# Order of the background work in a decoder step: selections ahead of row products, two groups of sparse tokens, a later first product

## The chip, the core and the metric

The kernel runs on one core of a Trainium2 chip. The core has five engines with a queue of instructions each: TensorE (PE, matrix products; PEld is its weight load), VectorE (DVE), ScalarE (ACT), GpSimd (POOL) and SyncE (SP, which here only issues DMAs). Each takes its queue strictly in order; semaphores hold an instruction until what it needs is done. All DMAs, issued from the queues of SP, ACT and POOL, run on 16 DMA engines. The metric is the device time of one execution in microseconds; the median of several is given. "Half" below is one step of the kernel's main loop, explained there.

## The reference

One layer of a decoder is computed for 256 prompt tokens and 8 sample tokens (264 columns). The part that matters is the PEER layer behind the first normalization: each token's query scores two sets of 128 keys for each of 8 heads, the best 16 pairs of a head choose 16 of 16384 single-neuron experts, and

```python
def block(args):
    xb, ib, gb = args
    hid = jax.nn.gelu(jnp.einsum('td,thkd->thk', xb, u_tab[ib]).astype(jnp.float32), approximate=False)
    coef = (gb * hid).astype(xb.dtype)
    return jnp.einsum('thk,thkd->td', coef, v_tab[ib])
```

So a token takes 8 x 16 = 128 rows of `u_tab` and 128 rows of `v_tab`, each of 2048 floats. Ahead of it come the mixers (an SSD scan, a short convolution, branch gates, an output projection), behind it a second normalization and a gated projection.

## The kernel before

**The main loop.** Everything with a weight matrix runs through one list, `order`, of weight tiles of 128 x 1024 floats: "halves". For each half SP loads the tile (`fetch`, L135), ACT rounds it to fp32r (`whi`, L146) and DVE takes the rest (`wlo`, L147), and PE multiplies with both. Loads go out four halves ahead and splits three halves ahead (`next_half`). Stage by stage: 24 column blocks of convolution inputs, the short convolution, the gates, the output projection, the queries; then **u**, 128 blocks of two halves, which multiplies the first 216 tokens with all 16384 experts' u rows (L271 to L274, `pair_block`); then **v**, 8 chunks of 16 blocks of two halves, which multiplies the coefficients of all experts with the v rows; then the last projection.

**Two ways through PEER.** The first 216 tokens (TD) are computed densely: all 16384 hidden values, times a gate that is zero where an expert isn't chosen. The last 48 (NSP: 40 prompt tokens and the 8 samples) are computed sparsely: only their chosen rows are gathered from HBM. Both need the selection first.

**The background planner.** What isn't the main loop is written as Python generators in a list, `tasks`, whose place in it is their rank. Behind each half the kernel calls `tick(budget)`. A tick first runs what was deferred to it (`defer`), then goes through `tasks` in order: a task that isn't waiting may emit work as long as the credit is above zero; `yield 2.4` takes 2.4 credits, `yield ("w", n)` lets it wait for n ticks. Credit comes back by the budget at each tick (1.1 in u, 1.0 in v) and may run below zero. So the planner sets, at build time, at which half each instruction enters its engine's queue; the engines then work through the queues. `Grid` spaces the steps of a task: at least n ticks behind the last step's planned time, and at least one tick from now.

**The tasks of this case**, all started around the queries' end:

- `token_rows` transposes x1 of the 48 sparse tokens to rows and writes them to HBM (`x1_d`).
- `select_all` runs three selections (`select`): tile 0, the prompt tokens 128 to 255; tile 1, the 8 samples, laid out as 64 rows of token and head; tile 2, the prompt tokens 0 to 127. Selections are DVE work: sums of candidates, top 16 (L1040 to L1044), lookups (`big`, L1071 to L1076). Behind tiles 0 and 1 `send` writes the chosen rows' numbers and weights of the sparse tokens to HBM (L1132). Behind tile 0 the task `gates(128, 88)` is put at the head of the list, and at the very end `select_all` itself goes on as `gates(0, 128)`, once the first gates are done (L1111 to L1113).
- `gates` builds, four tokens a step and a step every three halves, two one-hot matrices: four POOL instructions (L1151) and one of DVE (L1152); six halves later PE multiplies them (`gps`, L1164) and ACT copies the result to `gs`. Behind 32 tokens SP writes `gs` (2 MB) to HBM (L1156).
- `sparse_experts` runs through 96 jobs: for each group of tokens, first the u rows, then the v rows. Job by job POOL gathers 128 rows (`ug`, L1188, two buffers, the next job's gather ahead of a product), and a product on DVE follows every four halves: for u the dot products with `x1s` (L1216), for v the sum into `x1s` (L1226). Ahead of a group's first product `x1s` must be filled: the group's n token rows, 128/n times (L1207); `x1s` has one buffer, which the group before gives up only when PE has folded its 128 partial sums to n tokens (`yS`, L1232). `index` loads a tile's row numbers from HBM.
- Behind the last gates, `to_v` frees the selection's buffers and starts `residual` (copies for v's accumulators) and `prep(0)`: for each of a chunk's four blocks, load gates and hidden values, multiply, split into `co` (L1301 to L1311). v's first chunk needs all four; later chunks are prepared beside the one before, and what is left of `prep` at a chunk's start is run out without matmuls between. Before the last chunk the kernel emits what is left of `sparse_experts` (L1395), since its result enters the second normalization.

The sparse tokens form three groups, `GR`: 32 prompt tokens, 8 prompt tokens, and the 8 samples. When tile 0 is sent, `sparse_experts` is put at the head of `tasks`, so that from then on products rank above `select_all`. Job 32 (the first v row of the first group) waits until tile 1 is sent, and loads its index.

Of the kernel before, what the change touches and what calls it, by code (L numbers as in the profile page):

```python
# [10 lines left out]
F = mybir.dt.float32  # L11
R = mybir.dt.float32r
U32 = mybir.dt.uint32
# [6 lines left out]
NS = 8  # L20
T = PT + NS
TW = T + 2
NSP = 48
# [7 lines left out]
PH = 8  # L31
TOPK = 16
# [13 lines left out]
TB = 32  # L46
NB, TR = divmod(TD, TB)

GR = ((0, 32, 0, 88, 32), (32, 8, 0, 120, 8), (40, 8, 1, 0, 64))


@with_exitstack
def hybrid_step(ctx: ExitStack, tc: tile.TileContext, xT, pT, w_in, w_dt, w_bs, w_bc, w_o, w_q, w_pg, w_pp,
                uT, vP, uR, vR, keysT, par, hpar, hist, h0, eye, tri, iota, fold, yT, o_hp, o_hs, o_cp, o_cs, o_sp, o_ss):
    nc = tc.nc
    te, ve, ac, gp, sy = nc.tensor, nc.vector, nc.scalar, nc.gpsimd, nc.sync
# [4 lines left out]
    dram = ctx.enter_context(tc.tile_pool(name="dram", bufs=1, space=bass.MemoryType.DRAM))  # L61
# [36 lines left out]
    def bank(name, tag="bg", bufs=4):  # L98
        return psum.tile([128, 512], F, name=name, tag=tag, bufs=bufs)
# [12 lines left out]
    sidx = cpool.tile([128, NSP], U32, name="sidx")  # L112
    scf = cpool.tile([128, NSP], F, name="scf")
# [38 lines left out]
    tasks = []  # L152
    later = []
    clock = {"t": 0, "credit": 0.0, "in": False}

    def defer(n, fn):
        later.append((clock["t"] + n, fn))
# [31 lines left out]
    def spawn(gen):  # L189
        tk = {"gen": gen, "wait": 0}  # L190
        tasks.append(tk)
        return tk
# [130 lines left out]
    for q in range(6):  # L323
        n = min(3, 16 - 3 * q)
# [8 lines left out]
        for s in range(n):  # L333
            h, l = split_block(xt[:, s * T:(s + 1) * T], "x")
# [622 lines left out]
    DONE = {}  # L957
# [130 lines left out]
    def select_all():  # L1088
        while sum(h in DONE for h in range(PH)) < PH:
            yield ("w", 1)  # L1090
        t2_stack.close()
        sp = P["sp"] = sp_stack.enter_context(tc.tile_pool(name="select", bufs=1))
        P["oh"] = oh_stack.enter_context(tc.tile_pool(name="onehot", bufs=1))
        for t, (t0, n, nh) in enumerate(TT):
            sel = sp.tile([128, 3, nh * TOPK], F, name=f"sel{t}")
            yield from select(t, sel)
            if t < 2:
                send(sel, t, nh)
            if t == 0:
                tasks.insert(0, {"gen": sparse_experts(), "wait": clock["t"] + 1})  # L1100
            if t != 1:
                nd = min(n, TD - t0)
                yield ("w", 2)
                ps = bank("slt")
                for q in range(3):
                    te.transpose(ps[:, q * 128:q * 128 + n], sel[:n, q], ident[:n, :n])
                for q in range(3):
                    ac.copy(slot[q][:, t0:t0 + nd], ps[:, q * 128:q * 128 + nd])
                if t == 0:
                    tasks.insert(0, {"gen": gates(t0, nd), "wait": clock["t"] + 1})  # L1110
        while "G" + str(PT // 2) not in DONE:  # L1111
            yield ("w", 1)
        yield from gates(0, PT // 2)  # L1113


    sx_d = [dram.tile([128, n], U32, name=f"sx{g}_d") for g, (_, n, _, _, _) in enumerate(GR)]
    sg_d = [dram.tile([128, n], F, name=f"sg{g}_d") for g, (_, n, _, _, _) in enumerate(GR)]
    x1_d = dram.tile([NSP, D], F, name="x1_d")

    def send(sel, t, nh):  # L1120

        sp = P["sp"]
        ix = sp.tile([128, nh * TOPK], U32, name=f"ix{t}")
        fx = sp.tile([128, nh * TOPK], F, name="fx", tag="fx", bufs=1)
        n = TT[t][1]
        ve.scalar_tensor_tensor(fx[:n], sel[:n, 0], 128.0, sel[:n, 1], OP.mult, OP.add)
        ve.tensor_copy(ix[:n], fx[:n])
        for g, (_, m, tile_, lo, r) in enumerate(GR):
            if tile_ == t:
                c = nh * TOPK // m  # L1130
                for d, src in ((sx_d[g], ix), (sg_d[g], sel[:, 2])):
                    gp.dma_start(out=bass.AP(tensor=d.tensor, offset=d.offset, ap=[[m, r], [r * m, c], [1, m]]),  # L1132
                                 in_=src[lo:lo + r].rearrange("p (c m) -> p c m", m=m))
        DONE["sent%d" % t] = True

    GS = {}

# [40 lines left out]
        gp.dma_start(out=x1_d, in_=xr[:NSP])  # L1178

    def sparse_experts():  # L1180
        jobs = [(tab, k0, n, c) for k0, n, _, _, _ in GR for tab in (uR, vR) for c in range(k0, k0 + n)]
        rows = {}

        def get(i):
# [4 lines left out]
                                      in_offset=bass.IndirectOffsetOnAxis(ap=sidx[:, c:c + 1], axis=0))  # L1189
                rows[i] = t  # L1190

        def index(t):
            for g, (k0, n, tile_, _, _) in enumerate(GR):
                if tile_ == t:
                    gp.dma_start(out=sidx[:, k0:k0 + n], in_=sx_d[g])
                    gp.dma_start(out=scf[:, k0:k0 + n], in_=sg_d[g])

        yield ("w", 1)
        index(0)
# [2 lines left out]
        for i, (tab, k0, n, c) in enumerate(jobs):  # L1202
            ks = slice(k0, k0 + n)
            if tab is uR and c == k0:
                x1s = lp.tile([128, D], F, name="x1s", tag="x1s", bufs=1)
                for q in range(128 // n):
                    gp.dma_start(out=x1s[q * n:(q + 1) * n], in_=x1_d[ks])  # L1207
            if i == 32:
                while "sent1" not in DONE:
                    yield ("w", 1)  # L1210
                index(1)
            get(i + 1)
            yield grid(STEP)
            t = rows.pop(i)
# [256 lines left out]
def _inputs(x_prompt, x_sample, p_prompt, p_sample, state_ssm, state_ssd_conv, state_shortconv,  # L1471
# [34 lines left out]
        iota=np.tile(np.arange(128, dtype=np.float32), (128, 1)),  # L1506
        fold=np.concatenate([np.tile(np.eye(g[1]), (128 // g[1], 1)) for g in GR], 1).astype(np.float32),
    )
# [33 lines left out]
```

## Time and profile before

| | |
|---|---|
| median of 3 runs | 2680.55 us (2678.95 to 2682.51) |
| profiled execution | 2681.55 us, its span 2679.8 us |
| granted clock of TensorE, mean | 0.984 |
| packets of DMA | 677.84 MB, 253 GB/s over the span |
| gathers of `ug` | 48 of u rows, median 8.7 us to landing; 48 of v rows, 9.2 us |
| loads of weights in u and v | 256 of 512 KB each, 5.4 and 5.9 us |

The u stage lies about from 1150 to 1860 us of the span, v from there to 2500 us. The page gives busy times and idle times of engines; the windows view gives them for stretches of the span, also for one line alone, where the counts (x) tell how fast that line went; the waits view tells who waited for whom; the timeline gives single instructions, in square brackets how long their engine was idle before and what ended that.

### The profile page before, as it was taken

The page shows a single profiled execution, that of the slowest core. Times are in us where ns is not written, and L with a number is a line of the kernel's source. Part 1 is how long each engine was busy: PE and PEld are TensorE (multiplying, and loading weights), DVE is VectorE, ACT ScalarE, POOL GpSimd, SP SyncE. Part 2 cuts the span into 40 slices and gives each one's busy share as a digit, 9 for nine tenths or more (in the row PEclk, how much of TensorE's full clock was granted, in tenths as well). Part 3 has the DMA queues.
Part 4 walks back from the last instruction along what each step waited for, and adds up shares of the span by engine and source line. Part 5 has one row for each costly group of instructions (what it writes and reads, how often), then busy time and mean ns, then how long its engine had stood idle before and what let it go on. Part 6 is the DMA issues. An engine that isn't in the chain of part 4 may idle for free.

```text
span 2679.8 us, 48780 instructions
## 1 busy us (share of the span) xinstructions
PE 2605.1 (97%) x18999; PEld 2549.7 (95%) x18999; DVE 2039.8 (76%) x3258; ACT 1343.0 (50%) x1894; POOL 739.7 (28%) x802
## 2 busy tenths in 40 slices
PE   8999999999999999999999999997889989999999
PEld 8999999999999999999899999997779989999999
DVE  7899865566445577899788887776869978877886
ACT  5665533454334445655565565555434434444563
POOL 2232200000000010100699478784332332100100
PEclk9999999999999999999999999998889999999999
DMA  6798756556666666667898998889879989887664
GB/s 229 225 298 265 246 166 181 182 174 183 180 182 181 180 181 174 176 203 207 264 326 328 349 334 328 330 334 342 331 268 366 378 310 366 308 267 243 204 197 136
DMA packets 202041, 677.84 MB, mean 253 GB/s; under 512 B 23712, under 2 KB 61216, under 8 KB 188192
## 3 DMA queue, kind: packets, MB, share of 16 engines
q1 hardware_dynamic: 156128, 509.65, 58.7%
q0 software_dynamic: 27664, 146.49, 15.1%
q10 hardware_dynamic: 18016, 18.58, 2.0%
q8 instruction: 148, 2.42, 0.4%
q14 instruction: 85, 0.70, 0.1%
HBM read 633.72 MB, written 40.90 MB: 252 GB/s over the span
## 4 chain that ended last, share of the span: by engine, by line
PE 82%; POOL 6%; DMA 5%; DVE 4%; issue 2%; ACT 1%; SPq 0%; DVEq 0%; ACTq 0%; POOLq 0%
PE mm L271 22%; PE mm L237 15%; PE mm L235 15%; PE mm L236 15%; PE mm L272 11%; POOL o L1151 5%; DMA w<-uT 2%; PE mm L274 1%; DVE wlo L147 1%; PE gps L1164 1%; DMA x1s<-x_d 1%; POOL ug L1188 1%; DMA ug<-uR,sidx 1%; DMA al<-a_d 1%; PE yS L1232 0%
## 5 line engine op out<-in xcount | busy, mean ns | idle before, releaser
L147 DVE TENSOR_TENSOR wlo<-w,whi 128x1024 fp32r<-128x1024 f32 x916 | 1115.9, 1223 | 405.9 <-ACT whi L146 401.3
L146 ACT CAST whi<-w 128x1024 fp32r<-128x1024 f32 x916 | 961.0, 1051 | 841.5 <-PE mm L236 289.6
L271 PE MATMUL mm<-co,whi 128*128 128x432 f32 x1920 | 613.8, 377 | 23.4 <-DVE co L1311 15.1
L271 PE MATMUL mm<-x,whi 128*128 128x432 f32 x1920 | 610.4, 375 | 1.1 <-ACT whi L146 1.1
L237 PE MATMUL mm<-x,wlo 128*128 128x264 f32 x1920 | 550.0, 286 | 2.7 <-DVE wlo L147 2.7
L235 PE MATMUL mm<-x,whi 128*128 128x264 f32 x1920 | 549.7, 286 | 1.5 <-ACT whi L146 1.5
L236 PE MATMUL mm<-x,whi 128*128 128x264 f32 x1920 | 547.3, 285 | 0.0
L272 PE MATMUL mm<-co,wlo 128*128 128x216 f32 x2048 | 524.6, 266 | 14.8 <-DVE wlo L147 14.8
L272 PE MATMUL mm<-x,wlo 128*128 128x216 f32 x2048 | 521.3, 265 | 14.8 <-DVE wlo L147 14.7
L272 PEld LDWEIGHTS mm<-co,wlo 128*128 128x128 f32 x2048 | 397.6, 194 | 17.4 <-DVE wlo L147 15.6
L272 PEld LDWEIGHTS mm<-x,wlo 128*128 128x128 f32 x2048 | 393.7, 192 | 21.0 <-DVE wlo L147 19.0
L271 PEld LDWEIGHTS mm<-co,whi 128*128 128x128 f32 x1920 | 368.3, 192 | 42.8 <-DVE co L1311 16.5
L271 PEld LDWEIGHTS mm<-x,whi 128*128 128x128 f32 x1920 | 364.0, 190 | 17.6 <-ACT whi L146 1.5
L235 PEld LDWEIGHTS mm<-x,whi 128*128 128x128 f32 x1920 | 363.6, 189 | 3.2 <-ACT whi L146 1.8
L237 PEld LDWEIGHTS mm<-x,wlo 128*128 128x128 f32 x1920 | 362.4, 189 | 3.1 <-DVE wlo L147 3.1
L236 PEld LDWEIGHTS mm<-x,whi 128*128 128x128 f32 x1920 | 363.6, 189 | 0.0
L1151 POOL TENSOR_SCALAR o<-iot,slot,slot 128x128 f32<-128x128 f32 x216 | 354.1, 1646 | 1.6
L1216 DVE SCALAR_TENSOR_TENSOR ug<-ug,x1s 128x2048 f32<-128x2048 f32 x48 | 110.3, 2297 | 44.2 <-DMA x1s<-x_d 31.8
L1188 POOL DMA_INDIRECT ug<-vR,sidx x48 | 78.7, 1640 | 219.9 <-DVE x1s L1226 167.5
L833 POOL CAST r1h<-r1gbh 128x2 fp32r<-128x2 f32 x16 | 5.2, 326 | 476.3 <-PE mm L237 476.3
L1188 POOL DMA_INDIRECT ug<-uR,sidx x48 | 72.7, 1514 | 162.1 <-DVE ug L1216 133.6
L1226 DVE SCALAR_TENSOR_TENSOR x1s<-ug,scf,x1s 128x2048 f32<-128x2048 f32 x45 | 105.5, 2345 | 2.7 <-DMA ug<-vR,sidx 2.7
(350 smaller groups left out, 3864.3 us busy)
## 6 DMA issues: line engine op xcount, KB each, us to landing
w<-uT SPq DMA_DIRECT2D x256, 512.0 KB, 5.4
w<-vP SPq DMA_DIRECT2D x256, 512.0 KB, 5.9
w<-w_in SPq DMA_DIRECT2D x240, 512.0 KB, 3.9
w<-w_bc SPq DMA_DIRECT2D x32, 512.0 KB, 3.7
w<-w_bs SPq DMA_DIRECT2D x32, 512.0 KB, 3.6
w<-w_o SPq DMA_DIRECT2D x32, 512.0 KB, 3.6
w<-w_q SPq DMA_DIRECT2D x32, 512.0 KB, 3.6
w<-w_pg SPq DMA_DIRECT2D x32, 512.0 KB, 4.3
```

The lines of the kernel that those rows point to most:

```text
L146: ac.copy(hi, w)
L147: ve.tensor_tensor(lo, w, hi.bitcast(F), OP.subtract)
L235: te.matmul(ps, wh, xh[kb], start=(first and q == 0), stop=False)
L236: te.matmul(ps, wh, xl[kb], start=False, stop=False)
L237: te.matmul(ps, wl, xh[kb], start=False, stop=(last and q == n - 1))
L271: te.matmul(ps, hi[:, ws], xp[kb], start=(kb == 0), stop=False)
L272: te.matmul(ps[:, :TD], lo[:, ws], xp[kb][:, :TD], start=False, stop=False)
L274: te.matmul(ps, hi[:, ws], xp[kb], start=False, stop=True)
L1151: gp.tensor_scalar(o1[:, q], iot, slot[0][:, c], slot[2][:, c], OP.is_equal, OP.mult)
L1188: gp.indirect_dma_start(out=t, out_offset=None, in_=tab, in_offset=bass.IndirectOffsetOnAxis(ap=sidx[:, c:c + 1], axis=0))
L1216: ve.scalar_tensor_tensor(t, t, 1.0, x1s, OP.mult, OP.mult, accum_out=shid[:, c:c + 1])
L1226: ve.scalar_tensor_tensor(x1s, t, scf[:, c:c + 1], x1s, OP.mult, OP.add)
```

## The change

Three things, in the planner's inputs and in the way the indices travel:

1. `sparse_experts` is appended to `tasks` instead of put at the head, so it ranks below `select_all` and, when they come, above `prep`. The first gates are still put at the head.
2. `GR` has two groups, 32 and 16 tokens. The second holds 8 prompt tokens and the 8 samples. Its row numbers come from two tiles into one tensor of HBM: the prompt tokens' part is written at once by POOL (as before), the samples' part by 16 DMAs on SP's queue (8 heads, numbers and weights), deferred by two ticks behind tile 1's selection. `index(1)` then loads the whole second group.
3. Behind the loads of `x1s` the generator waits four ticks before it goes on to the next gather and the first product.

```diff
-GR = ((0, 32, 0, 88, 32), (32, 8, 0, 120, 8), (40, 8, 1, 0, 64))
+GR = ((0, 32), (32, 16))
...
             if t == 0:
-                tasks.insert(0, {"gen": sparse_experts(), "wait": clock["t"] + 1})
+                spawn(sparse_experts())
...
-        for g, (_, m, tile_, lo, r) in enumerate(GR):
-            if tile_ == t:
-                c = nh * TOPK // m
-                for d, src in ((sx_d[g], ix), (sg_d[g], sel[:, 2])):
-                    gp.dma_start(out=bass.AP(tensor=d.tensor, offset=d.offset, ap=[[m, r], [r * m, c], [1, m]]),
-                                 in_=src[lo:lo + r].rearrange("p (c m) -> p c m", m=m))
-        DONE["sent%d" % t] = True
+
+        def rows(eng, g, tok, src, stride, runs, m):
+            for d, x in ((sx_d[g], ix), (sg_d[g], sel[:, 2])):
+                eng.dma_start(out=bass.AP(tensor=d.tensor, offset=d.offset + tok * m,
+                                          ap=[[m, len(src)], [stride, runs], [1, m]]),
+                             in_=x[src.start:src.stop].rearrange("p (c m) -> p c m", m=m))
+
+        if t == 0:
+            for g, (k0, m) in enumerate(GR):
+                lo = n - (NSP - NS) + k0
+                src = range(lo, min(lo + m, n))
+                rows(gp, g, 0, src, m * m, 128 // m, m)
+        else:
+            g, m = len(GR) - 1, GR[-1][1]
+
+            def later_rows():
+                for h in range(PH):
+                    rows(sy, g, h * m + m - NS, range(h * NS, h * NS + NS), m * m, 1, m)
+                DONE["sent"] = True
+
+            defer(2, later_rows)
...
-        def index(t):
-            for g, (k0, n, tile_, _, _) in enumerate(GR):
-                if tile_ == t:
-                    gp.dma_start(out=sidx[:, k0:k0 + n], in_=sx_d[g])
-                    gp.dma_start(out=scf[:, k0:k0 + n], in_=sg_d[g])
+        def index(g):
+            k0, n = GR[g]
+            gp.dma_start(out=sidx[:, k0:k0 + n], in_=sx_d[g])
+            gp.dma_start(out=scf[:, k0:k0 + n], in_=sg_d[g])
...
                 for q in range(128 // n):
                     gp.dma_start(out=x1s[q * n:(q + 1) * n], in_=x1_d[ks])
+                yield ("w", 4)
             if i == 32:
-                while "sent1" not in DONE:
+                while "sent" not in DONE:
                     yield ("w", 1)
                 index(1)
```

More of the change, by code (lines that the diff above doesn't have):

```diff
@@ L1113, in select_all @@
         yield from gates(0, PT // 2)
-    sx_d = [dram.tile([128, n], U32, name=f"sx{g}_d") for g, (_, n, _, _, _) in enumerate(GR)]
-    sg_d = [dram.tile([128, n], F, name=f"sg{g}_d") for g, (_, n, _, _, _) in enumerate(GR)]
+    sx_d = [dram.tile([128, n], U32, name=f"sx{g}_d") for g, (_, n) in enumerate(GR)]
+    sg_d = [dram.tile([128, n], F, name=f"sg{g}_d") for g, (_, n) in enumerate(GR)]
     x1_d = dram.tile([NSP, D], F, name="x1_d")
@@ L1180, in sparse_experts @@
     def sparse_experts():
-        jobs = [(tab, k0, n, c) for k0, n, _, _, _ in GR for tab in (uR, vR) for c in range(k0, k0 + n)]
+        jobs = [(tab, k0, n, c) for k0, n in GR for tab in (uR, vR) for c in range(k0, k0 + n)]
         rows = {}
```

## The prediction

> **What bounds the kernel now.** I read the page first: busy shares, the 40 slices, the chain.
>
> ```profile
> span 2679.8 us, 48780 instructions
> PE 2605.1 (97%) x18999; PEld 2549.7 (95%) x18999; DVE 2039.8 (76%) x3258; ACT 1343.0 (50%) x1894; POOL 739.7 (28%) x802
> PE   8999999999999999999999999997889989999999
> PE 82%; POOL 6%; DMA 5%; DVE 4%; issue 2%; ACT 1%; SPq 0%; DVEq 0%; ACTq 0%; POOLq 0%
> L272 PE MATMUL mm<-x,wlo 128*128 128x216 f32 x2048 | 521.3, 265 | 14.8 <-DVE wlo L147 14.7
> ```
>
> PE bounds the kernel nearly everywhere, so a change in the background order can only pay where PE stands still: the slices with 7 and 8 behind the middle. To find these places I count one line. Each weight half of the u and v stages holds eight matmuls of L272 (2048 in the 256 halves of u). The windows view of that line alone, in 50 us stretches, is a speedometer (the last columns are granted clock, DMA share, GB/s):
>
> ```profile
> 1300.00:1350.00 50.00, 32.07 (x122) 24.56 (x123) 0.93 0.86 290
> 1400.00:1450.00 50.00, 35.98 (x143) 27.11 (x143) 1.00 0.87 301
> 1500.00:1550.00 50.00, 40.10 (x160) 30.27 (x159) 1.00 0.99 370
> 1850.00:1855.00 5.00, 2.51 (x8) 1.95 (x8) 0.82 1.02 407
> 1855.00:1860.00 5.00, 3.63 (x13) 3.04 (x14) 0.84 1.01 385
> 1850.00:1900.00 50.00, 16.67 (x53) 14.18 (x54) 0.62 0.85 314
> 1950.00:2000.00 50.00, 31.80 (x123) 24.27 (x122) 0.90 0.79 272
> 2000.00:2050.00 50.00, 33.85 (x129) 26.12 (x129) 0.90 0.89 327
> 2100.00:2150.00 50.00, 40.92 (x163) 30.82 (x162) 1.00 0.98 378
> 2150.00:2200.00 50.00, 31.38 (x120) 24.04 (x120) 0.90 0.82 293
> ```
>
> Undisturbed, v does 163 per 50 us, so a half takes 2.45 us, even with the DMA engines at 0.98. With gate matmuls between, u does 143, so three halves take 8.4 us. The places that are short: **A**, 1300 to 1350, (143-122)/143 x 50 = 7.3 us; **B**, 1850 to 1900, (163-53)/163 x 50 = 33.7 us; **C**, 1950 to 2050, (40+34)/163 x 50 = 22.7 us; **D**, 2150 to 2200, 13.2 us. In all 77 us, the clock's half speed after each stop included.
>
> Next I asked what PE waits for there, with the waits view and the timeline:
>
> ```profile
> DVE ug L1216 <- DMA x1s<-x_d: 8.4, 1, 8.4
> DVE ug L1216 <- DMA x1s<-x_d: 23.4, 2, 12.2
> 1987.44 5.71 POOL L1207 DMA_DIRECT2D x1s<-x_d  x11 [15.02 <-PE yS L1232]
> 1995.42 2.83 POOL L1207 DMA_DIRECT2D x1s<-x_d  x5 [2.28 <-DMA x1s<-x_d]
> 2004.06 2.29 DVE L1216 SCALAR_TENSOR_TENSOR ug<-ug,x1s 128x2048 f32<-128x2048 f32 x1 [11.25 <-DMA x1s<-x_d]
> 1869.25 0.70 PE L271 MATMUL mm<-co,whi 128*128 128x432 f32 x1 [8.30 <-issue]
> 1878.37 0.73 PE L271 MATMUL mm<-co,whi 128*128 128x432 f32 x1 [6.53 <-DVE co L1311]
> 1886.06 0.73 PE L271 MATMUL mm<-co,whi 128*128 128x432 f32 x1 [5.06 <-DVE co L1311]
> 1891.98 0.73 PE L271 MATMUL mm<-co,whi 128*128 128x432 f32 x1 [3.29 <-DVE co L1311]
> ```
>
> A, C and D are one thing three times: a group's first product stands on VectorE before its x1s has landed (8.4 us in u; 23.4 us for the two later groups, the first row from 1250 to 1550, the second from 1850 to 2330). VectorE works in order, so the weight splits (L147) queue behind that product, and PE runs dry. B is the passage from u to v: PE takes up v's first four coefficient blocks one by one, as L1311 delivers them, because their preparation begins only when the last gate is written.
>
> **The change part by part.** Positions are halves of u and v (256 each), counted by the planner's rules: 1.1 credits per half of u, 1.0 in v.
>
> *Rank.* A selection of eight heads costs 1.1 + 8 x 0.95 + 1.4 + 4 x 3.4 + 0.8 = 24.5 credits, the small one 6.65. The first ends at half 51 in both kernels. Before, the remaining 31.2 credits share the halves with 22 gate steps (15.4) and 22 products (52.8): 99.4 / 1.1 = 90 halves, so selection ends at 144. The gates of the first tile are done at 121 (22 steps of 3 halves), and those of the second, 32 x 3 = 96 halves, run from 148 to 244. With the write and its deferral `to_v` comes at 250, six halves before u ends: only the first of the four co blocks is begun in u. After, no product runs before the selections end: (31.2 + 12 x 0.7) / 1.1 = 36 halves, so half 89. Now the first tile's gates are last, at 120; the second's follow at once and end at 216, and `to_v` comes at 222. `prep` takes 8 halves a block beside the products: multiplies at 227, 235, 243 and 251, last co at 255, u's end at 256. So B's wait goes. The trace shows the hole that closes, in the windows view of L1151:
>
> ```profile
> 1450.00:1500.00 50.00, 37.31 (x17) 1.00 0.92 345
> 1500.00:1550.00 50.00, 0.00 (x0) 1.00 0.99 370
> 1550.00:1600.00 50.00, 34.60 (x19) 1.00 0.94 335
> ```
>
> From 1500 to 1550 POOL builds no gate at all: it waits for the selection. What stays of B is the cost of the last gate write, seen in 1850 to 1860 as 10 - 21/3.26 = 3.6 us (3.26 is 163/50), now near half 222, and about 1 us at the boundary. **B gains 33.7 - 3.6 - 1 = 29.**
>
> *The wait of four halves.* The first product of a group now comes five halves behind its loads, 12.3 us. Behind the waiting generator nothing is queued on an engine; it only emits later. For A the loads go out near half 59 and the product at 89, so that wait goes entirely. **A gains 6** (7.3, less about 1 for POOL, held for the index at half 59, below).
>
> *Two groups for three.* One transition goes, with its 16 loads, its fold and its gelu; the other has 8 loads of 128 KB for 16 of 64 KB.
>
> ```profile
> x1s<-x_d POOLq DMA_DIRECT2D x32, 64.0 KB, 5.5
> x1s<-x_d POOLq DMA_DIRECT2D x4, 256.0 KB, 11.1
> L1232 PE MATMUL yS<-fld,x1s 128*128 128x8 f32 x32 | 3.6, 253 | 0.0
> ```
>
> Eight issues take 8 x 0.52 = 4.2 us (5.71 for eleven), with no pause as behind the eleventh. A landing of 128 KB is between 5.5 and 11.1; I take 5.5 as nearer (64 KB), so 9.7 us, inside 12.3. At 11.1 it is 15.3, 3 us late, about a half that the splits made ahead mostly hide. The transition falls at half 337, inside a chunk, where before both fell on chunk boundaries. Left are the fold's 3.6 us and some 1.3. **C and D gain 35.9 - 3.6 - 1.3 = 31.** The 96 products are the same; the last group ends at half 457 for 416, and the last chunk, which needs it, starts at 480. With products v runs 163 per 50 us, so 41 more such halves cost nothing.
>
> *The row writes on SP.* At half 63 sixteen DMAs of 512 bytes stand before weight loads on SP's queue. Nearest rows:
>
> ```profile
> L643 SPq DMA_DIRECT2D h0t<-h x64: 378/384/874, 84.3 to 295.5; - x64
> SPq L1156 <- ACT gs L1165: 40.0, 6, 7.4
> g_d<-gs SPq DMA_DIRECT2D x6, 2048.0 KB, 11.3
> acs_d<-acs SPq DMA_DIRECT2D x1, 32.0 KB, 1.5
> sx_d<-ix POOLq DMA_DIRECT2D x2, 4.0 KB, 5.7
> ```
>
> Issue is 16 x 0.384 = 6.1 us. SP runs ahead, so it may also wait for VectorE's ix, up to 7.4 us as it waits for gs; the deferral by two halves cuts that. A gate write holds SP for 6.7 us on average and puts 11.3 us of transfer before the weights, 18 in all, and costs PE at most the 3.6 above; so about 14 us hide. Cost between 0 and 4; I take **-2**.
>
> *POOL while selection is denser.* From the lines view of 1300 to 1500 and of 1550 to 1840, and the timeline of the first index:
>
> ```profile
> L1151 POOL TENSOR_SCALAR o<-iot,slot,slot 128x128 f32<-128x128 f32 x88 | 160.9, 1835 | 0.6
> L1188 POOL DMA_INDIRECT ug<-uR,sidx x17 | 24.5, 1440 | 7.8 <-DVE ug L1216 4.9 <-issue 2.3 <-DVE big L1071 0.3
> L1151 POOL TENSOR_SCALAR o<-iot,slot,slot 128x128 f32<-128x128 f32 x128 | 193.2, 1517 | 1.1
> 1291.57 0.58 POOL L1195 DMA_DIRECT2D sidx<-sx_d  x1 [1.51 <-DMA sx_d<-ix]
> 1297.41 2.01 POOL L1207 DMA_DIRECT2D x1s<-x_d  x4
> ```
>
> A gate step needs 4 x 1.835 = 7.3 us of POOL per 8.4 us, with three quarters of a gather (1.1) it is full. After, halves 53 to 89 have steps without gathers (7.3 of 8.4), later ones steps beside gathers at 1.517 (7.2 of 8.4). The index and loads hold POOL for 1299.4 - 1291.6 = 7.8 us at half 59, against 6 halves of lead (16.8 us) less 7.3 for the step: just hidden. Cost 0 to 11, I take **-2**.
>
> Sum: 6 + 29 + 31 - 2 - 2 = 62 us. The profiled execution took 2681.55 us, 1.75 above its span and 1.0 above the median of the three runs; so from 2680.55 I predict **2619**.
>
> **The rivals.**
>
> *POOL becomes the bound* (slower than forecast). For: both tiles' gates now follow without a hole, and 17 of its instructions took 37.31 us in 1450 to 1500, 2.19 each. At that, a step is 8.8 us, with gathers 9.9: 12 steps x 0.4 + 10 x 1.5 = 19 us, 17 more than I took: 2636. Against: 1.517 where no selection runs.
> The Trainium skill (GPSIMD Engine Reference, section Key points) says that GpSimd shares its SBUF interfaces with VectorE and contends with instructions of two SBUF inputs; selection is full of these, which speaks for this rival in halves 53 to 89. The trace agrees as far as 1835 beside 1517 ns goes.
>
> *DMA at halves 222 to 256.* Prep's two tiles of 128 x 864 floats per 8 halves (864 KB in 19.6 us, 45 GB/s) join u's 370 GB/s at a share of 0.99. If all of it is above what the engines can do, 34 halves x 2.45 x 45/370 = 10 us: 2629. Against: v carries the same loads at 163 halves' matmuls.
>
> *The rank changes nothing*, because something other than selection holds the second tile's gates: B's 29 stay, 2648. Against: the x0 row.
>
> *The sixteen row writes go one after another* (slower than before). If each waits until the one before has landed, as two writes into one DRAM tile may, SP stands for 16 x 5.7 = 91 us at the landing of sx_d, 14 hidden: 77, so 2619 + 75 = 2694. It decides from (64 + 14)/16 = 4.9 us each; at SP's own 1.5 it is 24 - 14 = 10: 2627. Against: the x1s loads into one tile, eleven without a pause.
> By the Trainium skill (DMA: Bandwidth & Descriptors, section Anatomy of one DMA) a DMA has a fixed cost of about 2.0 us, stated for GpSimd's path; by that estimate it would be 32 - 14 = 18, so 2635. No row here shows such a chain.
>
> **How the numbers follow.** Forecast 0.69; POOL 0.12; DMA 0.06; rank without effect 0.04; serial writes 0.09, of it 0.05 slower, 0.02 the same, 0.02 faster. Faster by over 0.2% (5 us, about what a measurement of this kernel can tell from no change): 0.69 + 0.12 + 0.06 + 0.04 + 0.02 = 0.93; same 0.02; slower 0.05. The low end takes every stall whole but the fold: 77 - 3.6 = 73, rounded to 75 for the POOL lag of 1350 to 1400: 2605. The high end is the rank rival with a little more, 2650; beyond it lie the serial writes, and some of the forecast's own misses, under 0.2 in all.
>
> **What would show it.** Right: L1151 without an empty stretch, ending some 42 halves, 100 us, before u ends; the co blocks made beside u's matmuls and no PE gap at the passage; no wait of L1216 for x1s above 3 us; two folds; L272 near 163 in all of v but one stretch. Wrong: SP standing at the row writes and L146 waiting for w near half 63; PE waiting for gps from 1300 to 1500; a wait for the first product of the second group.

## The result and the profile after

| | before | after |
|---|---|---|
| median of 4 runs each, on the same chip | 2681.53 us (2678.95 to 2688.9) | 2612.81 us (2611.07 to 2615.31) |
| profiled execution, its span | 2681.55 us, 2679.8 us | 2611.91 us, 2610.1 us |
| mean granted clock | 0.984 | 0.998 |
| ratio of the times | | 0.974 (95%: 0.9719 to 0.9761) |

The forecast was 2619 us, the range 2605 to 2650; the kernel after came out 6 us below the forecast. The first part of the page of the kernel after (span; busy time, share and number of instructions of each engine), and from its second part the row of PE in 40 slices:

```profile
span 2610.1 us, 48704 instructions
PE 2579.9 (99%) x18967; PEld 2526.5 (97%) x18967; DVE 2033.3 (78%) x3256; ACT 1342.6 (51%) x1893; POOL 734.4 (28%) x774
PE   9999999999999999999999999999999999999999
```

The digits 7 and 8 behind the middle are gone. PE has 25 us less of busy time than before although 32 matmuls of 0.25 us are all that was taken away. In the stops of B the granted clock was 0.50 (kernel before, 1865 to 1895 us), and a matmul of L271 took 622 ns there (1869 to 1895) against 371 ns where nothing stopped (2100 to 2145). The lines view of these two windows:

```profile
L271 PE MATMUL mm<-co,whi 128*128 128x432 f32 x17 | 10.3, 622 | 23.2 <-DVE co L1311 14.9 <-issue 8.3
L271 PE MATMUL mm<-co,whi 128*128 128x432 f32 x137 | 42.9, 371 | 0.0
```

So a stall costs in the busy column too.

The speedometer of the prediction, eight matmuls of L272 a half, in windows of the kernel after (us; busy time and count on PE and on PEld; granted clock, DMA share, GB/s):

```profile
1300.00:1350.00 50.00, 35.24 (x139) 26.24 (x138) 1.00 0.76 233
1850.00:1900.00 50.00, 38.43 (x153) 28.79 (x152) 1.00 0.94 355
1950.00:2000.00 50.00, 41.02 (x163) 30.90 (x162) 1.00 1.01 394
2000.00:2050.00 50.00, 38.45 (x152) 28.96 (x152) 1.00 0.98 374
2150.00:2200.00 50.00, 40.58 (x162) 30.57 (x161) 1.00 0.97 371
```

A has 139 for 122, B 153 for 53, C and D are at 152 to 163 where 120 to 129 stood, and the clock is whole in all of them. Windows at fixed times compare different halves, though, as one kernel runs ahead of the other. So for the sizes I took from each trace when the last matmul (L274) of each block of two halves ended, and subtracted: how many us the kernel after is ahead of the kernel before, at the same half of u and v.

```
half             2    58    62    74   114   162   250   256   258   266   288   298   338   354   362   418   512
before      1150.3 1303.1 1322.8 1355.9 1470.4 1595.5 1842.2 1861.0 1894.6 1916.0 1970.5 2017.8 2117.1 2160.3 2189.6 2331.6 2564.5
after       1147.9 1300.7 1311.5 1347.2 1458.0 1590.4 1830.7 1845.5 1850.4 1873.4 1927.6 1954.8 2057.7 2098.8 2118.6 2257.9 2494.9
ahead          2.4   2.4  11.3   8.7  12.3   5.1  11.5  15.5  44.2  42.6  42.9  63.0  59.4  61.4  71.0  73.7  69.6
```

The 69.6 at the end are the whole difference of the profiled executions (2681.55 - 2611.91 = 69.6). A step of this row is a gain or a loss at its place. The dip from 12.3 to 5.1 at half 162 is an exception, and no stall: in halves 114 to 162 the kernel after runs 128 gate matmuls where the kernel before, which has its hole there, runs 48, and the kernel before runs the rest of them later. The 2.4 at u's start arose ahead of anything that was changed. In the executions below, which all run the same code up to there, u began between 4.3 us earlier and 2.9 us later than in that of before; that is the grain of a single profile. A step of 2 or 3 us in one row can be chance; e10, which is the kernel after once more, shows how much.

Of the gates, the windows of L1165 (L1151 before; busy time and count on POOL) show a stretch without a hole, and its end:

```profile
1500.00:1550.00 50.00, 39.45 (x23) 1.00 0.92 329
1700.00:1750.00 50.00, 38.85 (x21) 1.00 0.88 307
1750.00:1800.00 50.00, 0.00 (x0) 1.00 1.00 397
```

The last of them starts at 1741.8 us, at half 216 as the prediction had counted, some 100 us ahead of u's end (1845.5). At the passage, the waits view of the kernel after from 1840 to 1875 has one row in which PE waits in the middle of its work; the rows of DVE co are gone:

```profile
PE mm L272 <- DVE wlo L147: 2.6, 2, 1.5
```

And the one transition, on POOL and on DVE (timeline: start, us, engine, line, what, and the idle time before with its releaser):

```profile
2052.96 4.01 POOL L1220 DMA_DIRECT2D x1s<-x_d  x8 [11.77 <-PE yS L1246]
2057.27 1.11 POOL L1202 DMA_INDIRECT ug<-uR,sidx  x1 [0.30 <-DMA x1s<-x_d]
```

```profile
2067.65 0.61 DVE L1351 TENSOR_TENSOR acc<-mm,acc 128x432 f32<-128x432 f32 x1 [0.28 <-PE mm L274]
2068.17 2.28 DVE L1230 SCALAR_TENSOR_TENSOR ug<-ug,x1s 128x2048 f32<-128x2048 f32 x1
```

Eight issues took 4.01 us, the first product came 15.2 us behind the first of them, and no idle time stands in front of it: x1s had landed. The landings (7.4 us from issue in the median, 8.9 at most) were longer than the 5.5 us that the prediction took; the eighth came 12.3 us behind the first issue, where 9.7 had been reckoned. The waits view from 1850 to 2400 has no row of DVE waiting for x1s.

### The profile page after: what moved, and what is told of

Its sections match the earlier page's. It is cut to its first block, busy times and chain, and to the rows that moved or that the text cites. A ratio compares the mean times of both kernels' runs of the same rounds, so it can differ in the third digit from the quotient of the medians.

```text
span 2610.1 us, 48704 instructions
## 1 busy us (share of the span) xinstructions
PE 2579.9 (99%) x18967; PEld 2526.5 (97%) x18967; DVE 2033.3 (78%) x3256; ACT 1342.6 (51%) x1893; POOL 734.4 (28%) x774
## 4 chain that ended last, share of the span: by engine, by line
PE 90%; DVE 4%; DMA 4%; issue 1%; ACT 0%; SPq 0%; POOL 0%; DVEq 0%; POOLq 0%; ACTq 0%
PE mm L271 26%; PE mm L237 15%; PE mm L235 15%; PE mm L236 15%; PE mm L272 14%; DMA w<-uT 2%; PE mm L274 2%; PE gps L1178 2%; DVE wlo L147 1%; DVE x1s L1240 1%; DMA al<-a_d 0%; DMA ug<-vR,sidx 0%; ACT whi L146 0%; DMA ug<-uR,sidx 0%; PE scr L996 0%
## 5 line engine op out<-in xcount | busy, mean ns | idle before, releaser
L271 PE MATMUL mm<-x,whi 128*128 128x432 f32 x1920 | 607.1, 373 | 0.7 <-ACT whi L146 0.7
L271 PE MATMUL mm<-co,whi 128*128 128x432 f32 x1920 | 601.9, 371 | 3.5 <-DVE co L1325 3.5
L272 PE MATMUL mm<-x,wlo 128*128 128x216 f32 x2048 | 519.1, 264 | 7.6 <-DVE wlo L147 7.6
L272 PE MATMUL mm<-co,wlo 128*128 128x216 f32 x2048 | 518.4, 263 | 3.3 <-DVE wlo L147 3.3
L272 PEld LDWEIGHTS mm<-x,wlo 128*128 128x128 f32 x2048 | 391.4, 191 | 13.4 <-DVE wlo L147 11.3
L272 PEld LDWEIGHTS mm<-co,wlo 128*128 128x128 f32 x2048 | 390.5, 191 | 6.0 <-DVE wlo L147 4.3
L271 PEld LDWEIGHTS mm<-co,whi 128*128 128x128 f32 x1920 | 361.6, 188 | 21.9 <-DVE co L1325 5.1
L271 PEld LDWEIGHTS mm<-x,whi 128*128 128x128 f32 x1920 | 361.9, 188 | 16.5 <-ACT whi L146 0.9
L1165 POOL TENSOR_SCALAR o<-iot,slot,slot 128x128 f32<-128x128 f32 x216 | 360.2, 1676 | 24.3 <-PE gps L1178 20.7
L1202 POOL DMA_INDIRECT ug<-vR,sidx x48 | 84.4, 1759 | 292.7 <-DVE x1s L1240 218.7
L1230 DVE SCALAR_TENSOR_TENSOR ug<-ug,x1s 128x2048 f32<-128x2048 f32 x48 | 109.7, 2286 | 10.8 <-DMA ug<-uR,sidx 10.8
```

What stands on the lines that cost most here:

```text
L271: te.matmul(ps, hi[:, ws], xp[kb], start=(kb == 0), stop=False)
L272: te.matmul(ps[:, :TD], lo[:, ws], xp[kb][:, :TD], start=False, stop=False)
L1165: gp.tensor_scalar(o1[:, q], iot, slot[0][:, c], slot[2][:, c], OP.is_equal, OP.mult)
L1202: gp.indirect_dma_start(out=t, out_offset=None, in_=tab, in_offset=bass.IndirectOffsetOnAxis(ap=sidx[:, c:c + 1], axis=0))
L1230: ve.scalar_tensor_tensor(t, t, 1.0, x1s, OP.mult, OP.mult, accum_out=shid[:, c:c + 1])
```

## The experiments

Each kernel is the kernel before or after with the edit shown; each time is a median beside the kernel before on the same chip. For all of them I give the same row as above, as gains (+) or losses (-) on the profiled execution of before in six stretches: ahead of half 58, A (58 to 62), the stretch of the row writes (62 to 74), 74 to 250, B (250 to 266), and the rest of v with C and D (266 to 512).

```
                          to 58      A   62-74  74-250     B    C,D    sum    median us   ratio (95%)
after                      +2.4   +8.9    -2.6    +2.8  +31.1  +27.0  +69.6    2612.81     0.974  (0.9719 to 0.9761)
e1  rank alone             +2.6   +8.9    -0.8    +0.9  +32.3   +1.0  +44.9    2635.61     0.9812 (0.9791 to 0.9833)
e2  wait alone             +4.6   -0.2    -0.1    -3.4   +4.2  +13.9  +19.0    2666.65     0.9937 (0.9918 to 0.9957)
e3  groups alone           -0.3   -3.1     0.0    +0.4   -1.2  +19.7  +15.5    2663.69     0.9919 (0.9899 to 0.9939)
e4  after, no rank         +4.3   +3.7    -0.7    +1.9   +5.3  +27.9  +42.4    2645.88     0.9866 (0.9843 to 0.9888)
e5  after, no wait         +3.5   +9.0    -7.3    +4.3  +32.2  +17.2  +58.9    2630.31     0.9808 (0.9774 to 0.9843)
e6  after, three groups    +1.1   +9.0    -0.7    +3.6  +32.6   +7.4  +53.0    2627.41     0.9787 (0.9756 to 0.9818)
e8  e6, wait 8             -0.3   +9.0    -0.7    +8.6  +33.0   +6.5  +56.1    2624.99     0.9783 (0.9767 to 0.9799)
e12 e6, one load           +5.1   +9.0    -8.0    +1.4  +30.3  +19.5  +57.3    2625.94     0.9787 (0.975 to 0.9823)
e7  after, writes on POOL  -0.1   +9.0    -0.6    +5.4  +32.6  +27.7  +74.0    2609.35     0.972  (0.9685 to 0.9754)
e9  after, writes twice    +2.8   +9.0    -9.1    +6.9  +34.1  +24.3  +68.0    2616.26     0.9754 (0.974 to 0.9769)
e10 after, again           +5.5   +8.9    -5.7    +6.4  +33.3  +26.5  +74.9    2609.28     0.9747 (0.9724 to 0.9771)
e11 e7, again              -1.3   +9.0    -1.2    +4.5  +32.2  +26.4  +69.6    2611.92     0.9736 (0.9723 to 0.9749)
```

The rows of after and e10 are the same kernel. They differ by up to 3.6 us in a stretch and by 5.3 us in the sum.

**e1: the rank alone.** In the kernel before:

```diff
-                tasks.insert(0, {"gen": sparse_experts(), "wait": clock["t"] + 1})
+                spawn(sparse_experts())
```

> The kernel before with the rank alone changed: three groups, no wait of four. Theory: the rank moves the end of the selections from half 144 to 92, the gates' end from 244 to 216 and the passage to 222, so the whole passage stall (B, 31 us by the times of the blocks' last matmuls) and the first product's wait (A, 9 us) go; the two later transitions stay, 13 us each, but off the chunk boundaries (C, D together 32 before, 26 here). Time about 2681 - 31 - 9 - 6 = 2635. Rival, that the rank matters little and the waits for x1s were the loss: about 2672.

2635.61 us, as expected. The rank gives the whole of A and the whole of B, with no wait in the generator and three groups still: the window at the passage is full. C and D gain 1.0 us, where 6 were expected.

```profile
1850.00:1900.00 50.00, 39.45 (x156) 29.59 (x156) 1.00 0.97 368
2050.00:2100.00 50.00, 31.97 (x121) 24.57 (x122) 0.90 0.82 269
```

The second row is the stall of the old kind that stays, a transition near half 338; DVE waits in it and the next for x1s, in the waits view from 2050 to 2300:

```profile
DVE ug L1216 <- DMA x1s<-x_d: 24.1, 2, 12.7
```

**e4: after without the rank**, the same line turned back:

```diff
-                spawn(sparse_experts())
+                tasks.insert(0, {"gen": sparse_experts(), "wait": clock["t"] + 1})
```

> The changed kernel with sparse_experts back at the head of the tasks: two groups and the wait, without the rank. Theory: passage at half 246 with only the first co block's multiply in u, so B comes back but for some 5, and A with it: about 2613 + 26 + 9 = 2648. Rival, that the wait and the groups carry the change: within 10 us of the changed kernel.

2645.88 us. The passage is back, as the window of L272 and the waits view from 1840 to 1900 show:

```profile
1850.00:1900.00 50.00, 21.70 (x76) 17.50 (x76) 0.73 0.87 333
```

```profile
PE mm L271 <- DVE co L1325: 11.9, 3, 6.5
```

B gains 5.3 in place of 31.1, C and D gain as in the kernel after. The two experiments agree: B is the rank's. A was expected to come back whole, and 3.7 us of it stayed away. In the three kernels without the rank A changes by -0.2, -3.1 and +3.7 us (e2, e3, e4); why it differs among them was not looked into.

**e2: the wait alone.** In the kernel before, behind the loads of `x1s`:

```diff
                     gp.dma_start(out=x1s[q * n:(q + 1) * n], in_=x1_d[ks])
+                yield ("w", 4)
```

> The kernel before with the wait of four halves alone. Theory: the first products of the second and third group no longer stand for x1s (11.25 and 12.19 us of VectorE), so C and D shrink to a fold of 3.6 us each, a gain of some 24; A hardly moves, since the first product comes only one half later (58 for 57); the passage comes at 246 for 250 and B shrinks by some 5. About 2681 - 29 = 2652. Rival, that the rank carries everything: 2680.

2666.65 us (9 runs, 2659.11 to 2680.28), between the two. A is unchanged, and the later transitions are only half cured: the waits view of v has

```profile
DVE ug L1217 <- DMA x1s<-x_d: 13.2, 2, 8.4
```

where before had 23.4. So five halves are too little for 16 loads. e6, e8 and e12 ask why.

**e3: two groups alone**, that is, after without rank and without wait (`tasks.insert(0, ...)`, no `yield ("w", 4)`).

> The kernel before with two groups alone (and the row writes on SP, at half 77): one transition, one fold and 8 loads less. Theory: D goes (12 us), C keeps its wait, some 2 us shorter with 8 loads of 128 KB, and the row writes cost 2 to 3. About 2681 - 11 = 2670. Rival, that the number of groups is what made C and D: 2650.

2663.69 us, nearer to the theory (2670) than to the rival (2650). One transition is left in v, and DVE waits for x1s once, 6.6 us.

**e5: after without the wait.**

```diff
-                yield ("w", 4)
```

> The changed kernel without the wait of four halves. Theory: the one later transition has its first product one half behind the loads (338 for 337) instead of five, so VectorE stands for 8 loads and a landing, some 7 us, of which PE loses 5 to 8; A stays away, since the first group's product comes at half 88 anyway. About 2613 + 7 = 2620. Rival, that the wait also serves A: 2613 + 7 + 9 = 2629.

2630.31 us, the rival's number, but not for its reason: A stays away (+9.0), so the rank had removed that and not the wait. What came back lies in v: 6.3 us of DVE waiting for x1s in the second group, and a second loss that neither side had. Without the four ticks everything later moves, and the last fold falls on a boundary of two chunks (halves 448 to 450), where the matmuls around it stop:

```profile
2337.32 2.34 DVE L1239 SCALAR_TENSOR_TENSOR x1s<-ug,scf,x1s 128x2048 f32<-128x2048 f32 x1
...
2339.72 3.19 PE L1245 MATMUL yS<-fld,x1s 128*128 128x16 f32 x16 [2.96 <-DVE x1s L1239]
...
2347.40 1.05 ACT L146 CAST whi<-w 128x1024 fp32r<-128x1024 f32 x1 [9.52 <-PE mm L271]
```

PE stands 2.96 us for the last sum on DVE, folds, and ACT's next split comes 9.52 us late. The loss is 10.0 us from half 418 on (68.9 to 58.9 ahead), where the kernel after loses 4.1 (73.7 to 69.6). In the stretch of the row writes this profile loses 4.7 more than that of after; of that below. The profiled execution took 2622.70 us, the fastest of four and 7.6 below their median, so the profile accounts for 10.8 of the 17.5 us by which the medians differ, and the rest stays open.

**e6: after with three groups** (the kernel before with rank and wait).

> The changed kernel with the three groups of before (rank and wait kept, no row writes on SP). Theory: one fold more, 3.6 us, and 16 loads for 8 behind a lead of five halves (12.3 us against 13.5), so some 1 to 3 us of wait at each transition; the row writes' 2.6 us on SP are saved. About 2613 + 4 = 2617. Rival, that two groups are worth the 12 us of D: 2625.

2627.41 us: the rival. The timeline of POOL in the first of the two later transitions, and of DVE behind it:

```profile
2049.55 5.15 POOL L1207 DMA_DIRECT2D x1s<-x_d  x10 [11.32 <-PE yS L1233]
2054.92 0.52 POOL L1207 DMA_DIRECT2D x1s<-x_d  x1 [0.22 <-DMA x1s<-x_d]
2057.30 0.52 POOL L1207 DMA_DIRECT2D x1s<-x_d  x1 [1.86 <-DMA x1s<-x_d]
2058.79 0.52 POOL L1207 DMA_DIRECT2D x1s<-x_d  x1 [0.98 <-DMA x1s<-x_d]
2059.50 0.52 POOL L1207 DMA_DIRECT2D x1s<-x_d  x1 [0.19 <-issue]
2060.36 1.08 POOL L1207 DMA_DIRECT2D x1s<-x_d  x2 [0.34 <-DMA x1s<-x_d]
```

```profile
2072.95 2.29 DVE L1217 SCALAR_TENSOR_TENSOR ug<-ug,x1s 128x2048 f32<-128x2048 f32 x1 [8.10 <-DMA x1s<-x_d]
```

Behind the tenth issue POOL pauses until an earlier load lands. The sixteen issues take 11.9 us, and DVE gets x1s 23.4 us behind the first (2072.95 - 2049.55), against a lead of five halves, 12.3 us.

**e8: e6 with a wait of eight**, so that nine halves, 22 us, lie between.

```diff
-                yield ("w", 4)
+                yield ("w", 8)
```

> The kernel of e6 (three groups, rank and wait) with a wait of eight halves for four. In e6 each later transition still cost about 10 us at PE: 16 loads are issued with pauses behind the tenth and land 23.4 us behind the first, against a lead of 5 halves, 12.3 us. Theory: what two groups bring is the count of loads behind a given lead, not the group; with a lead of 9 halves, 22 us, both waits of 8 us go and each transition costs its fold, 3.6 us, so three groups come to 2627 - 13 = 2614, the changed kernel's time. Rival, that a transition costs its 10 us whatever the lead (the loads crowd out other transfers, or hold POOL): 2627.

2624.99 us, not told from e6. DVE waits for x1s nowhere, and the first transition costs 3.6 us (70.7 to 67.1 ahead of before, at halves 330 to 338). But the second loses 6.8 (halves 402 to 418, where the kernel after gains 3.1). The waits view of that place:

```profile
DVE al L1302 <- DMA al<-a_d: 10.2, 1, 10.2
...
POOL gl L1287 <- DMA x1s<-x_d: 2.2, 1, 2.2
```

The loads of `prep` stand on POOL's queue behind the x1s loads, and DVE, in order, now stands at prep's multiply. The wait changed its owner.

**e12: e6 with one load a group**: the same bytes by one DMA, which reads the 8 rows of a group sixteen times (and the first group's 32 rows four times). The expectation below speaks of 16 rows and eight DMAs; the kernel has 8 rows and sixteen.

```diff
-                for q in range(128 // n):
-                    gp.dma_start(out=x1s[q * n:(q + 1) * n], in_=x1_d[ks])
+                gp.dma_start(out=x1s, in_=bass.AP(tensor=x1_d.tensor, offset=x1_d.offset + k0 * D,
+                                                  ap=[[0, 128 // n], [D, n], [1, D]]))
```

> The kernel after with three groups of 16 and the wait of four halves, as e6, but each group's x1s is filled by one DMA that reads the 16 rows eight times, in place of eight DMAs (128/n). e6 took 2627.41 us; DVE waited 8.1 us for x1s in a transition, whose loads were issued with pauses. If the number of issues on POOL's queue makes that delay: the load lands within the five halves, no wait of DVE for x1s over 2 us, each later transition costs about 3.6 us as the kernel after's single one does, and with two folds more than no group at all the time is about 2614 us, near the kernel after's 2612.81. If the bytes (the same in both) or the engines' queues make it: the waits of 8 us stay, and the time is about 2627 us.

The time, 2625.94 us (2619.97 to 2632.76), is the rival's; the trace of the later transitions is the theory's. POOL issues once and is free, and the product follows without a wait for x1s:

```profile
2059.65 0.55 POOL L1206 DMA_DIRECT2D x1s<-x_d  x1 [10.93 <-PE yS L1233]
2060.50 1.26 POOL L1188 DMA_INDIRECT ug<-uR,sidx  x1 [0.30 <-issue]
2061.75 0.88 POOL L1286 DMA_DIRECT2D gl<-g_d  x1
```

```profile
2075.04 0.60 DVE L1338 TENSOR_TENSOR acc<-mm,acc 128x432 f32<-128x432 f32 x1
2075.56 2.28 DVE L1217 SCALAR_TENSOR_TENSOR ug<-ug,x1s 128x2048 f32<-128x2048 f32 x1
```

Both later transitions cost 3.5 us (halves 330 to 338 and 394 to 402), and C and D gain 19.5 in place of e6's 7.4. The two loads landed 10.0 and 9.7 us behind their issue. So the number of issues on POOL's queue made the transitions dear, not the bytes; that rests on this one profile, not on the time. What was won there went in u: 8.0 us at halves 62 to 74, in which ACT waits 13.5 us for w, and 3.3 at halves 178 to 194, where one gather lands late (DVE waits 7.1 us for ug). The first of these comes just behind the first group's x1s, now one DMA of 1 MB. It was issued at 1299.3 us and landed 30.2 us later, and the six loads of weights issued from 1299.9 to 1315.3 took 17.7 us in the median (11.8 to 20.6) to land; six issued in the same window in e6 took 5.0. That the one large DMA held the weights up fits these figures; it was not tried apart.

**e9, e7, e10, e11: the row writes.** e9 sends the sixteen DMAs twice, e7 sends them on POOL's queue, e10 and e11 repeat after and e7, five runs each.

```diff
                 for h in range(PH):
                     rows(sy, g, h * m + m - NS, range(h * NS, h * NS + NS), m * m, 1, m)
+                for h in range(PH):
+                    rows(sy, g, h * m + m - NS, range(h * NS, h * NS + NS), m * m, 1, m)
```

> The changed kernel with the 16 row writes issued twice, 32 DMAs on SP. Theory: each issue takes SP's time, about 0.34 us, while the weight loads behind it are already late by SP's 6 us for ix; another 16 add 5.5 us to SP's standing and, with no cover left, about as much to PE: between halves 58 and 82 it falls back by 8 us instead of 3, in all 2613 + 5 = 2618. Rival, that only the wait for ix counts: 2613, and 3 us between these halves.

```diff
-                    rows(sy, g, h * m + m - NS, range(h * NS, h * NS + NS), m * m, 1, m)
+                    rows(gp, g, h * m + m - NS, range(h * NS, h * NS + NS), m * m, 1, m)
```

> The changed kernel with the 16 row writes issued on POOL's queue instead of SP's. Theory: SP no longer stands 6 us for ix and 8.7 us for the issues, so the 2.6 us that PE falls back between halves 66 and 74 go, while POOL, which waits for PE there, hides 16 x 0.57 = 9 us. 2613 - 2 = 2611, and the blocks' times show it at half 74. Rival, that the 2.6 us come from the selection's work on VectorE: no difference.

> The changed kernel unchanged, beside e11 on one chip, so that the two can be compared within a few us: 2613, with 2 to 3 us lost between halves 62 and 74.

> The row writes on POOL, as in e7, beside the changed kernel on one chip. Theory: 3 to 5 us below it, 2609, with the difference made between halves 62 and 74. Rival, that e7's 3 us were the spread of the runs: equal within 1 us.

The stretch from 62 to 74 loses 2.6, 5.7 and 7.3 us with the writes on SP (after, e10, e5), 9.1 with twice as many, 0.6 and 1.2 with them on POOL, 0.7 or 0.8 in e1, e6 and e8, which have none on SP. So at this place they cost some 2 to 6 us. The place matters: e3 and e4 have the same sixteen writes on SP, at halves 74 and 72 because their selection ends later, and there the blocks up to half 86 took 4.9 us, or 5.8 with gate matmuls, as undisturbed ones do. And e12, without the writes, loses 8.0 in the stretch too, so late weights in these halves have another cause beside them. In the medians nothing is left of it: 2609.35 and 2611.92 on POOL, 2612.81 and 2609.28 on SP. Of the expectations, e7 with 2609.35 doesn't tell its theory (2611) from its rival (2613), e9 with 2616.26 (2613.53 to 2618.93) lies between its theory (2618) and its rival (2613), and e11 met neither side, being 2.6 us above e10. No version was measurably faster than the kernel after.

## Why the prediction was right

It read the right places: A, B, and C with D gained 8.9 + 31.1 + 27.0 = 67 us, and all else together 2.6. By its own steps:

| step | predicted | measured |
|---|---|---|
| A, x1s of the first group | 6 | 8.9 |
| B, the passage from u to v | 29 | 31.1 |
| C and D, the later transitions | 31 | 27.0 |
| row writes on SP | -2 | -2.6 |
| POOL while selection is denser | -2 | +2.8 (halves 74 to 250) |
| start of u, not in the sum | 0 | +2.4 |
| sum | 62 | 69.6 |

One thing is not like for like in these rows. The 29 of B already has 3.6 us taken off for the last gate write near half 222, and that place lies in the row 74 to 250: the blocks that end at halves 226, 228 and 230 took 6.9, 5.8 and 5.9 us in place of 4.9, 3.8 in all. Term by term B then measured 27.3 and the POOL step +6.6.

**A.** The size came from L272's count in 50 us, less 1 for POOL, and the stall itself was larger: blocks 30 and 31, halves 58 to 62, took 19.7 us before and 10.8 after. The step stood under "The wait of four halves", and that is the wrong owner: e1 cures A without a wait (+8.9), e2 doesn't cure it with one (-0.2; e4, with the wait and two groups, +3.7), e5 keeps the cure without it (+9.0). The sentence that the loads go out near half 59 and the product comes at 89 was right, and it is the rank that puts the product there.

**B.** Right in mechanism and, within 2 us, in size, and the counting of credits carried it: gates without a hole, last gate at half 216 and some 100 us ahead of u's end, no PE wait for co. The rank alone gives 32.3, and without it 5.3 is left.

**C and D.** The mechanism was right, the size 4 us off: the term "35.9" was what was lost in the windows of C and D, and 50 us there hold ordinary losses too. By the block times the two transitions of before cost 20.1 (halves 288 to 298) and 11.6 (346 to 362), 31.7 in all. Against them stand 3.5 us for the one transition of after (62.9 to 59.4 ahead, halves 322 to 338), against 3.6 + 1.3 predicted, and 1.0 more for its last fold (4.1, and 3.1 before): 27.2. That eight loads land in the time and 16 don't was argued from eleven issues without a pause; e6 shows the pause behind ten, and the profile of e12 that without the issues the delay is gone. The step claimed this as a saving of two groups, and it is: with three groups, and the rank and the wait kept, e6 takes 2627.41.

**The row writes.** The -2 fits the -2.6 of this profile, but e10, the same kernel, lost 5.7 there, above the 0 to 4 that had been allowed. SP did stand, though not for the transfers of the writes: the waits view of SP from 1300 to 1330 has

```profile
SPq L1131 <- DVE ix L1127: 6.1, 1, 6.1
...
SPq L1131 <- DMA w<-uT: 1.9, 1, 1.9
```

and the timeline shows the writes going out one behind the other:

```profile
1311.90 0.34 SPq L1131 DMA_DIRECT2D sx_d<-ix  x1
...
1320.23 0.29 SPq L1131 DMA_DIRECT2D sg_d<-sel  x1
```

Sixteen in 8.6 us, with one gap of 1.9, which ended with the landing of a weight. In e10 and e5 they took 10.4 and 13.0 us, with pauses of up to 3.7 that ended with a landing too, in e3 and e4 5.4 us without a pause. None of this is a landing behind each write: the rival of serial writes (2694) is out. The deferral by two halves, which the prediction thought would cut the wait for ix, left 6.1 us of it. Not all of that is extra: in e6 and e7, which have no row write on SP, a weight load stands there until the same ix instruction, for 4.9 and 4.4 us. ACT then waits 5.8 us for w in the kernel after (one of the signs called wrong), and PE loses 2.6.

**POOL.** Here the prediction failed, and by more than anywhere else (-2 said, +6.6 like for like): the sign of "POOL while selection is denser" was wrong, and the rival "POOL becomes the bound" with it. The lines view from 1300 to 1370 (count; busy us, mean ns; idle us before and its releaser), first of the kernel before, where selection and products share VectorE, then of the kernel after, where there is selection alone:

```profile
L1151 POOL TENSOR_SCALAR o<-iot,slot,slot 128x128 f32<-128x128 f32 x31 | 58.3, 1887 | 0.2
```

```profile
L1165 POOL TENSOR_SCALAR o<-iot,slot,slot 128x128 f32<-128x128 f32 x33 | 46.5, 1419 | 19.7 <-PE gps L1178 19.7
```

Without products a gate instruction takes 1419 ns in place of 1887, and POOL stands 19.7 us because it is ahead of PE. The prediction applied 1835 to the halves without gathers, though that row came from a stretch that had both, and so laid on the selection what came with the two together. For the later halves, with gathers and products but no selection, it took 1517; there the kernel after has more (1380 to 1600):

```profile
L1165 POOL TENSOR_SCALAR o<-iot,slot,slot 128x128 f32<-128x128 f32 x102 | 178.0, 1753 | 0.8
```

So both sizes were off, in opposite ways. Neither cost PE anything: in the waits view of PE, from 1300 us to the end of u, no gate matmul (gps) waits in either kernel, and PE waits only for splits. That is also where the gain lies. Over halves 74 to 214 PE waits for the split wlo seven times and 4.5 us before, twice and 0.4 us after (waits view of PE, 1356 to 1735 and 1347 to 1735). The block times say the same: an undisturbed block takes 4.93 us, and 5.82 with one step of eight gate matmuls. With as many of both taken off as there were, 7.9 us are left over in these halves in the kernel before and 1.0 in the kernel after; 2.9 with the rank alone (e1), 0.0 to 5.3 in all other kernels with the rank, and 7.3 to 12.4 in e2, e3 and e4 without it. So this gain goes with the rank too, and the prediction had no term for it.

**The other rivals.** "The rank changes nothing" (2648) is out by e1; that number came all the same when the rank was taken away (e4, 2645.88), as B's 29 said. "DMA at halves 222 to 256" (2629) is out by the count of L272: prep's loads do run beside u's at a share of 1.00 to 1.02, and from 1800 us to u's end the line still does 147 in 45 us, which is the undisturbed 163 in 50.

```profile
1800.00:1845.00 45.00, 36.93 (x147) 27.94 (x147) 1.00 1.02 399
```

That the sum came within 8 us is in part luck, since the misses cancel: like for like, POOL and A came out 8.6 + 2.9 = 11.5 better than said, B, C with D and the writes 1.7 + 4.0 + 0.6 = 6.3 worse, and 2.4 lie ahead of the change. By e10, misses of 2 or 3 us in one step are within what a second execution of the same kernel changes; those of POOL and of C with D are not so small.

## What to carry to other kernels

Where one engine is 97% busy, look for the few stretches in which it is not, count one of its lines there, and ask which in-order queue made it stand: here three of four places were one product on VectorE in front of the weight splits. In a planner by rank, put first what the next stage waits for (the selection, on which gates, coefficients and the passage hang), and last what has slack to its due time (the products, whose last group ended 41 halves later for about 1 us). Where loads are late, count the issues on the queue before the bytes, and when a wait is moved, look for the next instruction behind the same queue: e8 turned a wait for x1s into one for prep's loads and won nothing.

## What the runs showed of the hardware

**GpSimd beside VectorE.** A gate instruction on POOL (128 x 128 floats) takes 0.78 us when VectorE is nearly idle (2.34 us for three) and over three times that, on average, beside certain VectorE instructions (8.15 us for three). The two rows, from the timeline of POOL in the kernel after, and the first of what VectorE does during the second:

```profile
1323.18 2.34 POOL L1165 TENSOR_SCALAR o<-iot,slot,slot 128x128 f32<-128x128 f32 x3 [2.48 <-PE gps L1178]
...
1395.67 8.15 POOL L1165 TENSOR_SCALAR o<-iot,slot,slot 128x128 f32<-128x128 f32 x3
```

```profile
1394.94 1.56 DVE L147 TENSOR_TENSOR wlo<-w,whi 128x1024 fp32r<-128x1024 f32 x1
1396.41 0.68 DVE L1166 TENSOR_TENSOR o<-iot,slot 128x512 f32<-128x512 f32 x1
1397.02 1.21 DVE L147 TENSOR_TENSOR wlo<-w,whi 128x1024 fp32r<-128x1024 f32 x1
```

During the first, VectorE runs an instruction of 0.27 us and then stands (its next one starts at 1325.36, 1.99 us idle before it); during the second it is busy with splits and one-hot comparisons, and from 1401 us with a product, which all read two tensors. The Trainium skill (GPSIMD Engine Reference, section Key points) names VectorE instructions with two SBUF inputs as what GpSimd contends with, and the rows agree. What didn't hold was "selection is full of these": from 1300 to 1370 its MAX8, FIND_INDEX8 and MATCH_REPLACE8, which read one tensor, took 10.8 us, its wide lookups of two tensors (L1071, L1074) 6.0. How much each kind slows GpSimd was not tried apart, and the means don't sort by it alone: beside products without selection they were 1517 ns in the kernel before and 1753 in the kernel after.

**POOL's DMA issues** follow each other at 0.5 us up to the tenth or eleventh and then wait, 0.2 to 2.3 us each, for one of them to land (e6, e8 and the kernel before). The eight of the kernel after go out without a pause.

**The clock behind a stop** was 0.50 from 1865 to 1895 us of the kernel before, and whole in the windows of the kernel after where those stops are gone.
